# A one-core decoder layer: norm rows of six heads and three groups sent through DRAM, split squares, and four small reorderings

## The chip, the cores and the metric

The kernel runs on one core of a Trainium2 chip. The metric is device time in microseconds from launch to end; three runs of the kernel before gave 1294.66, 1294.87 and 1296.31 us, and the change is compared with their median. The core's engines are TensorE (PE, with its weight loads PEld), VectorE (DVE), ScalarE (ACT), GpSimd (POOL) and SyncE (SP, which here only issues DMAs). ACT and POOL issue DMAs too.

## The reference

One decoder layer on 512 tokens of width 1024, all in float32: a half-weighted SwiGLU FFN, a mixer, cross-attention into 256 memory tokens, a second FFN and a last norm. The change lies in the mixer, whose two halves end in an RMS norm each:

```python
y = y.reshape(bsz, seqlen, SSD_WIDTH) * jax.nn.silu(z.astype(jnp.float32))
yg = y.reshape(bsz, seqlen, SSD_GROUPS, SSD_WIDTH // SSD_GROUPS)
yg = yg * lax.rsqrt(jnp.mean(yg * yg, axis=-1, keepdims=True) + EPS)
y_ssd = yg.reshape(bsz, seqlen, SSD_WIDTH).astype(h.dtype) * ssd_norm_w
...
o = diff_attention(q, k, v, lam, rel_bias)
o = o * lax.rsqrt(jnp.mean(o * o, axis=-1, keepdims=True) + EPS)
y_attn = (o.astype(h.dtype) * subln_w * (1.0 - lambda_init)).reshape(bsz, seqlen, DA_WIDTH)
return jnp.concatenate([y_ssd, y_attn], axis=-1) @ w_out
```

So for each token there is one inverse root per attention head (8 heads, 128 channels each) and one per state-space group (4 groups, 256 channels each). The attention logits also get a bias that depends on the distance of the positions, from a table of 32 buckets for 8 heads.

## The kernel before

Activations lie transposed: a tile is 128 channels (partitions) by 512 tokens in float32. A product in full precision is made of three products in fp32r, a float32 form that TensorE streams one column per step: each operand is split into a high part (a copy rounded to fp32r, on ACT) and a low part (the difference, on DVE), and high x high, high x low and low x high are added up in PSUM. Weights come in by DMA from SP in tiles of 128 x 1024 (`wr`) and are split on the way (`wh`, `wl`, L155 and L156; in the output half of an FFN L1313 and L1315).

A norm needs, for each token, a factor that is the same in all 128 partitions: a row. Tokens are columns, so the kernel makes it in three steps. First a column: the sum of squares over channels for tokens on partitions (128 x 4). Then the inverse root on POOL (a power of -0.5). Then back to a row.

- In a state-space group (`group`, L1020 to L1035) the squares of two tiles are added on DVE. Four plain fp32 products with the 128 x 128 blocks of the squares as stationary operand and one column of ones give `pn` (L1026). `inv_rms_cols` (L363) gives the column. `row_of` (L370) splits the column, multiplies the identity by each half (`ndiag`, two 128 x 512 diagonals, on the engines that are passed in, here POOL for both) and multiplies ones by the diagonals (`nrow`, two products of 512 columns). DVE multiplies the two tiles by the row out of PSUM (L1033).
- In a head (`head`, L843 to L865) the output `of` is transposed in four blocks on TensorE (`ptk`), ACT squares each block and sums it along its free dimension, and since tokens are then on partitions DVE multiplies by the column directly (`on`). Four more transposes (`pot`) bring it back, and the split into `ya` applies the gain of the norm.

The order of the work is planned in the code. `Order` (L57) keeps a clock `t` that counts TensorE's expected time (each `mm`, `transpose` and product adds its share). Dense work, the projections, is a list taken in order; heads, groups, convolutions, the position table and the sums of weights for the second FFN are chains. A chain that does `yield 4.2` is taken up again when the clock has gone 4.2 us further, so that its small products stand between the dense ones; the table `W` holds these delays. Instructions of TensorE, DVE and ACT are placed by the planner of the framework with this order as priority; SP and POOL keep the written order exactly. `behind(list)` holds an instruction behind others in the plan.

Three more places are touched. `prepare` (L630) multiplies the table of biases by a selection matrix (`prel`), copies it (`hot`) and writes it to DRAM from ACT's queue; it runs beside the last third of the first FFN, and ACT's DMA reads it as `bias` for each head. In a group, the products `pf` and `py` of each of two halves wait the delay `gd`. In a head, the products `po` of the weights with the values wait `hs` behind the last transposes. All small tiles share a pool of 55 buffers of 128 x 512. POOL also issues the accumulating DMAs that form sums of weight blocks for the second FFN in DRAM (`block_sums_in_dram`, L1272).

Of the kernel before, what the change touches and what calls it, by code (L numbers as in the profile page):

```python
# [11 lines left out]
F32 = mybir.dt.float32  # L12
R32 = mybir.dt.float32r
AF = mybir.ActivationFunctionType
# [22 lines left out]

W = {"h0": 3.4, "hs": 3.3, "ht": 2.0, "hv": 2.08, "hp": 6.75}
W |= {"g0": 8.28, "gc": 0.75, "gx": 0.92, "gb": 2.59, "gs": 0.51, "gt": 2.0, "gd": 6.9, "gy": 0.38, "gq": 11.8, "gn": 1.5, "gr": 4.4}
W |= {"c0": 4.97, "cs": 3.0, "ct": 4.82}  # L40

SPLIT, AHEAD = 5, 2
# [58 lines left out]
def body(tc, a, dbg=None):  # L101
# [31 lines left out]
    def aux(s, shape=(P, T)):  # L133
        return aux_p.tile(list(shape), F32, tag="aux", name=nm(s))

    def dump(name, t):
        if dbg and name in dbg:
            nc.sync.dma_start(dbg[name], t.bitcast(F32) if t.dtype == R32 else t)
# [24 lines left out]
    def split(s, src, scale=None, half=False, n=T):  # L163
        if half:
            both = s2(s, R32, (P, 2, T // 2))
            hi, lo = both[:, 0], both[:, 1]
        else:
            hi, lo = s2(s + "h", R32, (P, n)), s2(s + "l", R32, (P, n))
        last[:] = [i.ins for i in split_into(hi, lo, src, scale)]
        return hi, lo  # L170
# [192 lines left out]
    def inv_rms_cols(ps, nb, scale, eps):  # L363
# [3 lines left out]
        G.tensor_tensor(col, v, mhalf[:, :nb], ALU.pow)  # L367
        return col

    def row_of(col, nb, first, second, apart):  # L370
        ch = tiny.tile([P, nb], R32, tag="ch", name=nm("ch"))
        first.tensor_copy(ch, col)
        cl = small("cl", nb)
        first.tensor_tensor(cl, col, ch.bitcast(F32), ALU.subtract)
        diags = []
        for eng, c in ((first, ch.bitcast(F32)), (second, cl)):
            diags.append(s2("ndiag", R32, (P, nb, P)))
            eng.tensor_tensor(diags[-1], ident[:, None, :].to_broadcast([P, nb, P]), c[:, :, None].to_broadcast([P, nb, P]), ALU.mult)
        yield apart
        pr = aux("nrow", (P, nb * P))  # L380
        with behind(list(newest_mm)):
            for j in range(2):
                mm(pr, ones_r, diags[j].rearrange("p a b -> p (a b)"), j == 0, j == 1)
        return pr
# [245 lines left out]
    def prepare():  # L630
        rel_far = small("rel_far", 64, bufs=1)[:8]
        V.memset(rel_far, MASKED)
        yield 9.0
        prel = aux("prel", (8, T))
        for i in range(2):
            mm(prel[:, i * H : (i + 1) * H], rel_sb, hot[i], True, True)
        for c in range(T, RW, 64):
            S.dma_start(rel_d[:, c : c + 64], rel_far)
        yield 1.5
        for i in range(2):  # L640
            S.activation(hot[i][:8], prel[:, i * H : (i + 1) * H], AF.Copy, scale=-8.0)
        yield 2.0
        for i in range(2):
            S.dma_start(rel_d[:, i * H : (i + 1) * H], hot[i][:8])
        hot.clear()
# [104 lines left out]
    def backwards(t):  # L750
        n = t.free_size()
        return bass.AP(t.tensor, t.offset + P - 1, [list(t.ap[0]), [P, n // P], [-1, P]])
# [14 lines left out]
    def head(hd, q, kq, bias):  # L767
        es, w0, w1 = {}, {}, {}
        sm = [small("sm", 4) for _ in range(2)]

        def scores(*blocks):
            ps = [aux("ps") for _ in range(2)]
            parts, to = {}, 0
            for i in blocks:
                n = P * (i + 1)
                parts[i] = slice(to, to + n)
                to += n
                for j, (u, w) in enumerate(((0, 0), (0, 1), (1, 0))):
                    for c in range(2):
                        pc = slice(64 * c, 64 * c + 64)  # L780
                        mm(ps[c][:, parts[i]], q[u][pc, i * P : (i + 1) * P], kq[w][pc, :n], j == 0, j == 2)
            for i in blocks:
                n = P * (i + 1)
                es[i] = []
                for c in range(2):
                    ec = s2("ec", shape=(P, n))
                    mn = small("mn", 1, bufs=8)
                    V.tensor_tensor_reduce(out=ec[:, :n], in0=ps[c][:, parts[i]], in1=bias[:, T - n :], scale=0.125, scalar=3e38, op0=ALU.add, op1=ALU.min, accum_out=mn)  # L788
                    S.activation(ec[:, :n], ec[:, :n], AF.Exp, bias=mn, scale=-1.0, accum_out=sm[c][:, i : i + 1])  # L789
                    es[i].append(ec)  # L790

        def combine(i):

            n = P * (i + 1)
            e = es[i]
            rc = small("rc", 1)
            V.reciprocal(rc, sm[1][:, i : i + 1])
            rl = small("rl", 1)
            V.scalar_tensor_tensor(rl, sm[0][:, i : i + 1], nlam, rc, ALU.mult, ALU.mult)
            V.scalar_tensor_tensor(e[0][:, :n], e[1][:, :n], rl, e[0][:, :n], ALU.mult, ALU.add)  # L800
            e.pop()

        def turn(j):
            n = P * (4 - j)
            pt = aux("pt")
            for i in range(j, 4):
                transpose(pt[:, (i - j) * P : (i - j + 1) * P], es[i][0][:, j * P : (j + 1) * P])
            if n <= T // 2:
                both = s2("wt", R32, (P, 2, n))
                w0[j], w1[j] = both[:, 0], both[:, 1]  # L810
            else:
                w0[j], w1[j] = s2("wt", R32, (P, n)), s2("wt", R32, (P, n))
            split_into(w0[j], w1[j], pt[:, :n])

        scores(3)
        yield W["hs"]
        scores(2)
        combine(3)
        yield W["hs"]
        scores(1, 0)  # L820
        combine(2)
        turn(3)
        yield W["hs"]
        combine(1)
        combine(0)
        turn(2)
        yield W["hs"]
        turn(1)
        yield W["ht"]
        turn(0)  # L830
        yield W["hs"]
        es.clear()
        while hd // 4 not in vs:
            yield 1.0
        v = vs[hd // 4]
        hs = slice((hd % 4) * P, (hd % 4 + 1) * P)
        po = aux("po")
        for n, (v_, w_) in enumerate(((0, w0), (1, w0), (0, w1))):
            for j in (0, 1, 2, 3) if n < 2 else (1, 2, 3, 0):
                mm(po[:, j * P :], v[j][v_][:, hs], w_[j], n + j == 0, n == 2 and j == 0)  # L840
        w0.clear()
        w1.clear()
        of = s2("of")  # L843
        S.activation(of, po, AF.Copy)
        yield W["hv"]
        pt = aux("ptk")
        for b in range(4):
            transpose(pt[:, b * P : (b + 1) * P], of[:, b * P : (b + 1) * P])
        ss = small("ss", 4)
        junk = s2("junk", shape=(P, P))  # L850
        for b in range(4):
            S.activation(junk, pt[:, b * P : (b + 1) * P], AF.Square, accum_out=ss[:, b : b + 1])
        ev = small("ev", 4)
        V.scalar_tensor_tensor(ev, sm[0], EPS, sm[0], ALU.mult, ALU.mult)
        V.scalar_tensor_tensor(ev, ss, 1.0 / P, ev, ALU.mult, ALU.add)  # L855
        rr = small("rr", 4)
        G.tensor_tensor(rr, ev, mhalf, ALU.pow)  # L857
        on = s2("on", shape=(P, 4, P))
        V.tensor_tensor(on, pt.rearrange("p (a b) -> p a b", b=P), rr[:, :, None].to_broadcast([P, 4, P]), ALU.mult)
        yield W["hp"]  # L860
        pt = aux("pot")
        for b in range(4):
            transpose(pt[:, b * P : (b + 1) * P], on[:, b])
        ya[hd] = split("ya", backwards(pt), wsub)
        dump(f"ya_{hd}", ya[hd][0])  # L865

    wcv = []
# [61 lines left out]
    def group(g, bt, ct, xs, zs):  # L929
# [52 lines left out]
        for j in range(2):  # L982
# [3 lines left out]
            for hh in range(2):  # L986
# [5 lines left out]
                    S.activation(r[:, c], r[:, c], AF.Relu, bias=cum[:, c, hd : hd + 1], scale=-1.0)  # L992
                S.activation(r, r, AF.Exp, scale=-1.0)
                V.tensor_tensor(r, r, cbm, ALU.mult)
            yield W["gd"] + (W["gt"] if j == 0 else 0.0)
            pf = aux("pf")
            with behind(list(newest_mm)):
                for c in range(1, 4):
# [18 lines left out]
        for j in range(2):  # L1017
# [2 lines left out]
            S.activation(q_, yz[j], AF.Square)  # L1020
            sq.append(q_)
        V.tensor_tensor(sq[0], sq[0], sq[1], ALU.add)
        yield W["gq"] + (1.2 if g == 2 else 0.0)
        pn = aux("pn", (P, 4))
        for b in range(4):
            mm(pn[:, b : b + 1], sq[0][:, b * P : (b + 1) * P], ones[:, 0:1], True, True)  # L1026

        rh = inv_rms_cols(pn, 4, 4.0 / (4 * 256), 4.0 * EPS)
        yield W["gn"]
        pr = yield from row_of(rh, 4, G, G, W["gr"])  # L1030
        for j in range(2):
            n = 2 * g + j
            V.scalar_tensor_tensor(yz[j], yz[j], par[:, C_SSD + n : C_SSD + n + 1], pr, ALU.mult, ALU.mult)  # L1033
            ys[n] = split("ys", yz[j])
            dump(f"ys_{n}", ys[n][0])  # L1035

# [587 lines left out]
```

## Time and profile before

| what | value |
|---|---|
| median of three runs | 1294.87 us |
| profiled execution, its own time | 1296.09 us |
| span of its trace | 1294.1 us |
| TensorE busy | 1281.5 us (99%), 7709 products |
| DVE busy | 971.9 us (75%) |
| ACT busy | 707.6 us (55%) |
| POOL busy | 118.0 us (9%) |
| granted clock of TensorE | 0.997 |
| DMA | 234.75 MB, mean 181 GB/s |

The mixer runs from about 360 to 840 us of the span: heads 0 to 3 at 410 to 494, group 0 at 499 to 551, heads 4 to 7 at 589 to 651, groups 1 to 3 at 655 to 804. A product's width in TensorE's stream is read from the chain of waits in order of time, since the ends of products in the trace are modelled and overlap. "Idle before" in brackets names what an engine waited for.

### The profile page before, as it was taken

What the parts mean: (1) busy time and instruction counts of PE and PEld (TensorE: products, weight loads), DVE (VectorE), ACT (ScalarE), POOL (GpSimd) and SP (SyncE); (2) the same over time, 40 slices, a digit from 0 to 9 for tenths busy, and PEclk for the clock granted to TensorE, in tenths of its full rate; (3) what the DMA queues carried; (4) which work ended last, traced back from release to release, by engine and by line L of the source; (5) the groups of instructions that cost most, each with busy time, mean ns of one, the idle gap of its engine ahead of it and who ended that gap; (6) DMA issues with size and microseconds to landing.
All of it is one profiled execution on the core that took longest, in us unless ns stands there. A gap on an engine that the chain in (4) does not pass through costs nothing.

```text
span 1294.1 us, 20089 instructions
## 1 busy us (share of the span) xinstructions
PE 1281.5 (99%) x7709; PEld 1123.7 (87%) x7709; DVE 971.9 (75%) x1549; ACT 707.6 (55%) x1203; POOL 118.0 (9%) x149
## 2 busy tenths in 40 slices
PE   9999999999999999999999999999999999999997
PEld 7889998998988778877888888889899999989995
DVE  6988898797876686567868696645678868877886
ACT  7545564565654564447644574435466646555554
POOL 1001010001101011101102011020001000000000
PEclk9999999999999999999999999999999999999998
DMA  9368677788875436653476567593249876666662
GB/s 331 101 170 209 187 199 199 226 208 227 272 232 155 131 66 169 224 163 96 107 211 187 151 163 227 193 234 107 66 132 255 210 221 184 191 189 190 180 201 92
DMA packets 69551, 234.75 MB, mean 181 GB/s; under 512 B 8192, under 2 KB 9696, under 8 KB 69104
## 3 DMA queue, kind: packets, MB, share of 16 engines
q1 hardware_dynamic: 53488, 180.91, 42.2%
q0 software_dynamic: 13168, 45.67, 19.9%
q10 hardware_dynamic: 2800, 6.91, 1.7%
q8 instruction: 60, 0.98, 0.3%
q14 instruction: 35, 0.29, 0.1%
HBM read 231.30 MB, written 48.29 MB: 216 GB/s over the span
## 4 chain that ended last, share of the span: by engine, by line
PE 82%; issue 12%; DMA 2%; ACT 1%; DVE 1%; POOL 1%; POOLq 0%; SPq 0%; ACTq 0%
PE qb L243 12%; PE pm L146 10%; PE qe L243 8%; PE qa L243 8%; PE pxbc L146 5%; PE ob L1327 5%; PE oa L1327 4%; PE oe L1327 4%; PE pcq L146 3%; PE pz L146 3%; PE pa L146 2%; PE pk L146 2%; PE pq L146 2%; PE pcv L146 2%; PE pv L146 2%
## 5 line engine op out<-in xcount | busy, mean ns | idle before, releaser
L155 ACT ACTIVATE wh<-wr 128x1024 fp32r<-128x1024 f32 (+1 forms) x245 | 251.2, 1028 | 235.2 <-PE qe L243 27.9
L156 DVE TENSOR_TENSOR wl<-wr,wh 128x1024 fp32r<-128x1024 f32 (+1 forms) x245 | 290.8, 1188 | 83.5 <-ACT wh L155 61.3
L1313 ACT ACTIVATE wh<-wr 128x1024 fp32r<-128x1024 f32 (+1 forms) x78 | 76.9, 987 | 68.4 <-PE ob L1327 19.5
L1315 DVE TENSOR_TENSOR wl<-wr,wh 128x1024 fp32r<-128x1024 f32 (+1 forms) x78 | 87.5, 1131 | 15.0 <-ACT wh L1313 13.1
L789 ACT ACTIVATE ec<-ec,mn 128x512 f32<-128x512 f32 (+3 forms) x64 | 35.4, 554 | 21.9 <-DVE mn L788 21.9
L788 DVE CUSTOM_DVE_ANT_0 ec<-ps,bias 128x512 f32<-128x512 f32 (+3 forms) x64 | 28.1, 486 | 14.8 <-PE ps L146 14.7
L252 POOL DMA_DIRECT2D wr<-in_f2q x11 | 9.7, 881 | 309.8 <-DMA wr<-in_f2q 156.2
L902 DVE SCALAR_TENSOR_TENSOR conv<-pxbc,par,conv 128x511 f32<-128x511 f32 (+2 forms) x48 | 35.7, 745 | 2.3 <-ACT conv L898 1.5
L367 POOL TENSOR_TENSOR ncol<-nv,mhalf 128x4 f32<-128x4 f32 (+1 forms) x9 | 9.7, 1077 | 294.1 <-DVE nv L365 266.5
L146 PE MATMUL pxbc<-hnl,wh 128*128 128x512 f32 x128 | 35.4, 403 | 0.0
L146 PE MATMUL pxbc<-hnh,wh 128*128 128x512 f32 x128 | 35.3, 400 | 0.0
L146 PE MATMUL pxbc<-hnh,wl 128*128 128x512 f32 x128 | 32.3, 393 | 0.0
L454 DVE TENSOR_TENSOR gate<-qb,row 128x512 f32<-128x512 f32 x19 | 13.2, 692 | 22.1 <-PE qb L243 22.1
L146 PEld LDWEIGHTS pxbc<-hnh,wl 128*128 128x128 f32 x128 | 23.8, 188 | 5.3 <-issue 0.3
L252 POOL DMA_DIRECT2D wr<-in_f1q x16 | 14.0, 875 | 152.8 <-DMA wr<-in_f1q 49.8
L146 PEld LDWEIGHTS pxbc<-hnl,wh 128*128 128x128 f32 x128 | 23.3, 188 | 4.8 <-issue 0.4
L146 PEld LDWEIGHTS pxbc<-hnh,wh 128*128 128x128 f32 x128 | 23.2, 189 | 4.5 <-issue 0.3
L455 ACT ACTIVATE gate<-gate 128x1024 f32<-128x1024 f32 x19 | 20.1, 1056 | 10.9 <-DVE gate L454 10.9
L146 PE MATMUL pv<-wh,hnh 128*128 128x512 f32 x64 | 25.3, 395 | 0.0
L146 PE MATMUL pv<-wh,hnl 128*128 128x512 f32 x64 | 25.2, 393 | 0.0
L155 ACT ACTIVATE s24h<-s 128x512 fp32r<-128x512 f32 x30 | 18.8, 627 | 9.0 <-DVE s L214 8.9
L857 POOL TENSOR_TENSOR rr<-ev,mhalf 128x4 f32<-128x4 f32 x8 | 8.3, 1035 | 161.3 <-DVE ev L855 161.3
(465 smaller groups left out, 3546.9 us busy)
## 6 DMA issues: line engine op xcount, KB each, us to landing
wr<-in_f2q SPq DMA_DIRECT2D x44, 512.0 KB, 4.8
wr<-in_f1q SPq DMA_DIRECT2D x40, 512.0 KB, 4.5
wr<-in_f1b SPq DMA_DIRECT2D x23, 512.0 KB, 5.7
isum<-in_f2q SPq DMA_DIRECT2D x22, 512.0 KB, 5.8
wr<-isum SPq DMA_DIRECT2D x22, 512.0 KB, 4.0
wsum<-in_f2b SPq DMA_DIRECT2D x20, 512.0 KB, 6.3
wr<-wsum SPq DMA_DIRECT2D x20, 512.0 KB, 4.7
wr<-in_f1q POOLq DMA_DIRECT2D x16, 512.0 KB, 7.2
```

The costliest lines, as they stand in the source:

```text
L146: newest_mm[:] = [nc.tensor.matmul(out, w, x, start=start, stop=stop).ins]
L155: S.activation(hi, src, AF.Copy),
L156: V.tensor_tensor(lo, src, hi.bitcast(F32), ALU.subtract),
L243: newest_mm[:] = [nc.tensor.matmul(out, w_[:, wc], xs[kp][which][x_], start=first and j == 0 and f == 0 and kp == 0, stop=j == 2 and kp == ...
L252: last_sum[:] = [G.dma_start(raw, m, accum_op=ALU.add).ins]
L455: S.activation(gate, gate, AF.Silu)
L788: V.tensor_tensor_reduce(out=ec[:, :n], in0=ps[c][:, parts[i]], in1=bias[:, T - n :], scale=0.125, scalar=3e38, op0=ALU.add, op1=ALU.min, ...
L789: S.activation(ec[:, :n], ec[:, :n], AF.Exp, bias=mn, scale=-1.0, accum_out=sm[c][:, i : i + 1])
L902: V.scalar_tensor_tensor(y[:, d:], ps[:, : T - d], par[:, cw + j : cw + j + 1], y[:, d:], ALU.mult, ALU.add)
L1313: high = S.activation(hi, raw, AF.Copy)
L1315: low = V.tensor_tensor(lo, raw, hi.bitcast(F32), ALU.subtract)
L1327: newest_mm[:] = [nc.tensor.matmul(ps, a_[:, ts], b_[:, ws], start=first and k == 0 and j == 0, stop=k == n - 1 and j == 2, skip_group_che ...
```

## The change

- Heads 0 to 2 and 4 to 6 (`hd % 4 < 3`) go to a new function `normed_far`: ACT squares the untransposed output, the square is split in fp32r, and eight products of two columns of ones with its blocks give the column of sums (`pon`). The power on POOL follows; then the column (128 x 4) is written to DRAM by a DMA from POOL, read back 8 us later by a second one that gives all 512 values to each partition (`row_by_dram`), and 12 us after that DVE multiplies `of` by gain and row. The eight transposes go. Heads 3 and 7 stay as they were, with their `po` 0.8 us later.
- All groups split the added squares and use eight such products in place of four in plain fp32. Groups 0 to 2 take the row through DRAM in place of diagonals and `nrow`. Group 3 keeps the diagonals, on DVE in place of POOL, and its `nrow` stands 0.8 us earlier.
- Group 2's second `pf`/`py` stand 0.5 us later.
- The position table's products stand 4 us later, and the copies of them are held behind the last split of weights.

```diff
+W |= {"hn": 4.2, "rw": 8.0, "rr": 12.0}
...
+    def row_by_dram(col, landed, read):
+        there = dram.tile([P, 4], F32, name=nm("there"))
+        G.dma_start(there, col)
+        yield landed
+        row = s2("far")
+        G.dma_start(row, bass.AP(there.tensor, there.offset, [[0, P], [1, 4 * P]]))
+        yield read
+        return row.rearrange("p (t b) -> p b t", b=4)
+
+    def blocks(t):
+        return t.rearrange("p (b t) -> p b t", b=4)
...
-        yield 9.0
+        yield 13.0
         prel = aux("prel", (8, T))
...
-        for i in range(2):
-            S.activation(hot[i][:8], prel[:, i * H : (i + 1) * H], AF.Copy, scale=-8.0)
+        with behind(list(recent)):
+            for i in range(2):
+                S.activation(hot[i][:8], prel[:, i * H : (i + 1) * H], AF.Copy, scale=-8.0)
...
-        yield W["hs"]
+        yield W["hs"] + (0.8 if hd % 4 == 3 else 0.0)
...
         S.activation(of, po, AF.Copy)
+        if hd % 4 < 3:
+            yield from normed_far(hd, of, sm[0])
+            return
...
+    def normed_far(hd, of, sums):
+        sq = s2("osq")
+        S.activation(sq, of, AF.Square)
+        sq = split("osq", sq)
+        yield W["hn"]
+        pon = aux("pon", (P, 4, 2))
+        for b in range(4):
+            for j in range(2):
+                mm(pon[:, b], sq[j][:, b * P : (b + 1) * P], ones_r[:, 0:2], j == 0, j == 1)
+        ev = small("ev", 4)
+        V.scalar_tensor_tensor(ev, sums, EPS, sums, ALU.mult, ALU.mult)
+        V.scalar_tensor_tensor(ev, pon[:, :, 0], 1.0 / P, ev, ALU.mult, ALU.add)
+        rr = small("rr", 4)
+        G.tensor_tensor(rr, ev, mhalf, ALU.pow)
+        row = yield from row_by_dram(rr, W["rw"], W["rr"])
+        on = s2("on")
+        V.scalar_tensor_tensor(blocks(on), blocks(of), wsub, row, ALU.mult, ALU.mult)
+        ya[hd] = split("ya", backwards(on))
...
-            yield W["gd"] + (W["gt"] if j == 0 else 0.0)
+            yield W["gd"] + (W["gt"] if j == 0 else 0.5 if g == 2 else 0.0)
...
+        sq = split("ysq", sq[0])
         yield W["gq"] + (1.2 if g == 2 else 0.0)
-        pn = aux("pn", (P, 4))
+        pn = aux("pn", (P, 4, 2))
         for b in range(4):
-            mm(pn[:, b : b + 1], sq[0][:, b * P : (b + 1) * P], ones[:, 0:1], True, True)
-
-        rh = inv_rms_cols(pn, 4, 4.0 / (4 * 256), 4.0 * EPS)
-        yield W["gn"]
-        pr = yield from row_of(rh, 4, G, G, W["gr"])
+            for j in range(2):
+                mm(pn[:, b], sq[j][:, b * P : (b + 1) * P], ones_r[:, 0:2], j == 0, j == 1)
+
+        rh = inv_rms_cols(pn[:, :, 0], 4, 4.0 / (4 * 256), 4.0 * EPS)
+        if g < 3:
+            pr = yield from row_by_dram(rh, W["rw"], W["rr"])
+        else:
+            yield W["gn"]
+            pr = blocks((yield from row_of(rh, 4, V, V, W["gr"] - 0.8)))
```

More of the change, by code (lines that the diff above doesn't have):

```diff
@@ L1022, in group @@
         V.tensor_tensor(sq[0], sq[0], sq[1], ALU.add)
+        sq = split("ysq", sq[0])
         yield W["gq"] + (1.2 if g == 2 else 0.0)
[L1024 removed]
+        pn = aux("pn", (P, 4, 2))
         for b in range(4):
[L1026 to L1030 removed]
+            for j in range(2):
[6 more added lines that the diff above has]
+            pr = blocks((yield from row_of(rh, 4, V, V, W["gr"] - 0.8)))
         for j in range(2):
             n = 2 * g + j
[L1033 removed]
+            V.scalar_tensor_tensor(blocks(yz[j]), blocks(yz[j]), par[:, C_SSD + n : C_SSD + n + 1], pr, ALU.mult, ALU.mult)
             ys[n] = split("ys", yz[j])
```

1 line of the change is left out of this document (added).

## The prediction, made before the change was run

> **What bounds the kernel now.** I read the page's busy table first, then the table of stretches, then the chain in order of time through the heads and the groups, and last the timeline around the few places where TensorE stands.
>
> ```profile
> span 1294.1 us, 20089 instructions
> PE 1281.5 (99%) x7709; PEld 1123.7 (87%) x7709; DVE 971.9 (75%) x1549; ACT 707.6 (55%) x1203; POOL 118.0 (9%) x149
> ```
>
> ```profile
> 560.00:650.00 90.00, 90.00 (x490) 71.31 (x490) 67.09 (x178) 53.14 (x145) 9.99 (x11) 1.00 0.42 110
> ```
>
> The second fence is the stretch with heads 4 to 7 (columns: PE, PEld, DVE, ACT, POOL busy with counts, granted clock, DMA share, GB/s). TensorE is busy in all of its 90 us at granted clock 1.00, while DVE works 67.09/90 = 75%, ACT 59% and POOL 11%. So an instruction taken off TensorE shortens the kernel by its place in TensorE's stream, an instruction taken off the others only by what TensorE now waits for them, and the price of everything the change adds to DVE, ACT, POOL and DMA is nothing until it makes TensorE late.
>
> **What TensorE pays for the parts that are exchanged.** The chain in order of time gives each part's width in TensorE's stream (start, width, what):
>
> ```profile
> 517.70 1.02 PE py L146 x16
> ...
> 592.34 0.44 PE ptk L150 x4
> ...
> 599.75 0.44 PE pot L150 x4
> ...
> 689.99 7.71 PE pxbc L146 x34
> 697.70 0.79 PE pn L146 x8
> 698.49 3.34 PE pxbc L146 x14
> ...
> 705.46 0.46 PE nrow L146 x2
> ```
>
> A 512-column product in the stream is 7.71/34 = 0.227 us. One head pays ptk and pot, 2 x 0.44 = 0.88 us. A group's pn is 0.79 us, and the 14 products behind it take 3.34 where 14 x 0.227 = 3.18 were due, so 0.79 + 0.16 = 0.95 us in all. Its nrow is 0.46 us.
>
> The new sums are eight products of two columns against 128x128 pieces of a square split in two fp32r tiles, for six heads and four groups alike. No product of that form is in the trace. What bounds it is the load of its stationary tile:
>
> ```profile
> L146 PEld LDWEIGHTS pn<-ones,ysq x32: 187/192/193, 540.2 to 795.2; 128*128 128x128 f32 x32
> L146 PEld LDWEIGHTS pm<-ysh,wh x64: 186/188/189, 792.0 to 833.5; 128*128 128x128 f32 x64
> L146 PEld LDWEIGHTS prel<-hot,rel_sb x4: 80/84/85, 310.5 to 310.9; 32*8 32x8 f32 x4
> ```
>
> An eight-column load takes 84 ns, a 128-column load 188 to 192, whether the tile is plain fp32 (ysq) or fp32r (wh): (188 - 84)/120 = 0.87 ns a column, 0.11 us for 128. The old pn is 32 records for 16 products, two loads each, and its eight records in 0.79 us stand 0.10 us apart, near that load and not near the one column that they stream. The new form has eight loads too. So I price the new sums at eight loads, 8 x 0.11 = 0.88 us. Bounds: above, the old pn's 0.95; below, py, whose sixteen products stand 1.02/16 = 0.064 us apart, so 8 x 0.064 = 0.51 us.
>
> The Trainium skill's page "TensorE: Matmul & The Clock Gate", section "Back-to-back issue gap", gives products of 1 to 64 columns about 60 cycles, 25 ns. By that alone the ten sums would cost an estimated 80 x 0.025 = 2.0 us; the pn row's 0.10 us contradicts it, and the same page's section "LDWEIGHTS (loading the stationary operand)" makes 128/1.2 = 107 ns of the load, with which the rows agree.
>
> Terms on TensorE, then:
> - Heads 0 to 2 and 4 to 6: minus 0.88, plus 0.88, six times: 0 (+0.4 at worst, -2.2 at best). Eight loads go for eight loads.
> - Groups 0 to 3: the fp32 pn goes, the split one with as many loads comes: 0 (4 x (0.51 - 0.95) = -1.8 at best).
> - Groups 0 to 2: nrow goes: 3 x -0.46 = -1.4 us. This is the only part of the exchange that surely shortens the stream: TensorE's instructions should go from 7709 to 7709 - 6 = 7703.
>
> **The four reorderings.** The timeline shows four places where TensorE really stands; each is what one small edit touches.
>
> ```profile
> 311.79 1.09 PE L1327 MATMUL oe<-wl,s31h 128*128 128x512 f32 x4
> 313.74 1.20 PE L1327 MATMUL ob<-wh,s24h 128*128 128x512 f32 x4 [0.86 <-ACT wh L1313]
> ```
>
> ```profile
> 311.56 0.64 ACT L641 ACTIVATE hot<-prel 8x256 f32<-8x256 f32 x2 [1.55 <-PE prel L146]
> 311.97 0.62 ACTq L644 DMA_DIRECT2D rel_d<-hot  x2
> 312.63 2.01 ACT L1313 ACTIVATE wh<-wr 128x1024 fp32r<-128x1024 f32 x2 [0.43 <-DVE wr L1365]
> ```
>
> ```profile
> 481.26 0.39 PE L146 MATMUL pxbc<-hnh,wh 128*128 128x512 f32 x1
> 482.04 0.86 PE L146 MATMUL po<-wt,vh 128*128 128x512 f32 x4 [0.39 <-ACT wt L155]
> ```
>
> ```profile
> 744.61 1.07 PE L146 MATMUL pz<-hnh,wl 128*128 128x512 f32 x4
> 745.84 0.88 PE L146 MATMUL py<-th,xdt 128*64 128x128 f32 x12 [0.16 <-DVE th L994]
> ```
>
> ```profile
> 801.83 2.41 PE L146 MATMUL pm<-ysh,wh 128*128 128x512 f32 x8
> ```
>
> The lost time is the next start less the last start and its due products. ob: 313.74 - (311.79 + 4 x 0.227) = 1.04 us. po of head 3: 482.04 - (481.26 + 0.23) = 0.55 us. py of group 2: 745.84 - (744.61 + 0.91) = 0.32 us. pm behind group 3's row: eight products, due in about 1.07 + 4 x 0.227 = 1.98, take 2.41: 0.43 us. Sum 2.3 us.
> - Position table: ACT waits 1.55 us for prel, copies it, issues two DMAs for 0.62 us, and only then splits the weights for ob. With prel 4 us later and the copies held behind that split, the 1.04 us goes; should the 0.43 us in that row be a true wait for DVE, 0.6 at least. The copies and the 0.62 us of issues come later on ACT, where they stand before other splits: 0 to 0.62 us comes back, I take 0.2. The table's first reader is the first head, well behind the first FFN, so lateness there costs nothing.
> - Head 3's products 0.8 us later, group 2's second product 0.5 us later: other products stand in front, 0.55 and 0.32 us are filled.
> - Group 3's diagonals go from POOL to DVE, 0.8 us earlier: -0.43 us.
>
> I credit all four, less 0.2: -2.1 us.
>
> **What lies beside TensorE.**
>
> ```profile
> L155 ACT ACTIVATE ysh<-y x8: 619/632/636, 549.7 to 803.5; 128x512 fp32r<-128x512 f32 x8
> L156 DVE TENSOR_TENSOR ysl<-y,ysh x8: 682/693/693, 550.4 to 804.1; 128x512 fp32r<-128x512 f32 x8
> ```
>
> Per head ACT drops four squares with their sums and gains one square and one copy; even without the four, 2 x 0.63 = 1.3 us a head lie in its idle 41%. DVE gains one subtraction, 0.69 us: 6 x 0.69 over the heads' stretches, covered by its idle quarter. From po to the sum the chain is now copy, square, split high, split low: 3 x 0.63 + 0.69 = 2.6 us, against a delay of 4.2: it fits unless the queues add 1.6 us. In a group 0.63 + 0.69 = 1.3 us come between the added squares and pn. In group 2 that is tight:
>
> ```profile
> 751.69 0.68 DVE L1022 TENSOR_TENSOR ysq<-ysq,ysq 128x512 f32<-128x512 f32 x1
> ...
> 754.18 0.95 PE L146 MATMUL pn<-ones,ysq 128*128 128x1 f32 x8
> ```
>
> The sum is ready at 752.37 and used at 754.18, 1.8 us, less 1.3 leaves 0.5, less than one more DVE instruction ahead in the queue. I put +0.3 us there (0 to 1.3).
>
> The row's way through DRAM is a pow, a write, a wait on POOL, a read and one DVE product:
>
> ```profile
> L857 POOL TENSOR_TENSOR rr<-ev,mhalf 128x4 f32<-128x4 f32 x8 | 8.3, 1035 | 161.3 <-DVE ev L855 161.3
> ```
>
> ```profile
> isum<-isum POOLq DMA_DIRECT2D x11, 512.0 KB, 9.4
> ...
> bias<-rel_d ACTq DMA_DIRECT2D x8, 256.0 KB, 3.9
> ```
>
> ```profile
> hb<-in_hb POOLq DMA_DIRECT2D x1, 16.0 KB, 7.2
> ```
>
> (Last column: us from issue to landing.) POOL does the pow in 1.04; the small write lands within 7.2, as hb does; the read of 256 KB in 3.9 to 9.4, as the bias rows or as a slow POOL transfer: at most 17.6 us and two issues, against 8 + 12 = 20 of allowance. The read waits on POOL for the write; behind it stand the accumulating DMAs, due only in the second FFN, and the next head's pow, which comes a head later. The result is needed late:
>
> ```profile
> 620.16 1.91 PE po L146 x12
> ...
> 660.23 2.29 PE pm L146 x10
> ```
>
> Head 6's po ends at 622.07; 4.2 + 20 later is 646.3, and its first reader, pm, starts at 660.23: 14 us of cover. Without that cover each row would cost what it is late. POOL loses the diagonals and gains two DMA issues a row; it is busy 11% of the stretch, so either is covered.
>
> **Sum.** 0 + 0 - 1.4 - 2.1 + 0.3 = -3.2 us; at the lower bounds of the sums it is -3.2 - 2.2 - 1.8 = -7.2, with the upper bounds of the heads, the table's wait and issues, and group 2 it is -3.2 + 0.4 + 0.4 + 0.4 + 1.0 = -1.0. The profiled execution took 1296.09 us, 2.0 above its span and 1.2 above the median of the three runs (1294.87). Against its own time: 1292.9; carried to the median: 1291.7.
>
> **Rivals.**
> - *Cheap small products.* If loads of fp32r tiles with little to stream run at py's pace or better, the time is 1294.87 - 7.2 = 1287.7. For it: py's row. Against: equal loads for wh and ysq. One in ten. The Trainium skill's issue gap, cited above, is this rival's rule.
> - *The waits come back elsewhere.* All delays are counted on the planner's own clock and ten blocks change their cost in it, so the order of all three queues shifts from 310 to 800 us. The four stalls found sum to 2.3 us; as many new ones leave the nrow term alone, 1293.5. For it: group 2's 0.5 us, the issues on ACT. Against: only four such stalls in the whole middle now. Three in ten.
> - *Late rows.* Landings at the upper ends, 7.2 + 9.4, with the pow and about 1 us of issue for each are 19.6 us; behind a POOL held by an accumulating DMA they pass 20. Then the row's product stands at the head of DVE's in-order queue with the weight splits behind it, and ACT's and DVE's splits come late. Nine rows, each 1 us late on TensorE, are +9 - 3.2 = +5.8: 1300.7; it decides from 3.2/9 = 0.36 us a row. The longer life of the held head output, split square and row in the pool of 55 buffers works the same way (a DMA waits for a buffer); no row shows its price. For it: 9.4. Against: 14 us of cover, DMA share 0.42. One in ten. The Trainium skill's page "DMA: Bandwidth & Descriptors", section "Specifications", says that pieces under 512 bytes are read, modified and written; the column is written in 16-byte pieces, and no DMA of before has them.
>
> **Chances and range.** Forecast, half: 1291.7, own range 1289.5 to 1293.9 (the bound of -1.0 above, half of the way to the cheap products below). The other halves: 0.1, 0.3, 0.1. Faster by over 0.2% (2.6 us, about what a measurement of this kernel can tell from no change) holds for most of the forecast (0.38), all of the cheap products (0.1) and a little of the returning waits (0.05): 0.53. Slower: late rows and the worst of the waits, 0.11. The same: 0.36. The range runs from the cheap products' 1287.7, rounded to 1287.5, to 1295.5, 2 us above the returning waits' 1293.5, since as many waits again may come.
>
> **What would show it.** TensorE with 7703 instructions; pon's eight products 0.8 to 1.0 us wide, as pn's; ob, po, py and pm without a gap at the four places; DVE waiting on no DMA for the row; pm after heads and groups starting no later than other work allows. The prediction is wrong if pon is under 0.6 us wide, if new gaps of over 0.3 us stand on TensorE between 310 and 800 us, or if DVE idles on a row's landing.

## The result, and the profile after

The changed kernel takes 1300.78 us (median of six runs, 1299.48 to 1303.38) against 1294.82 us for the kernel before (six runs, 1294.65 to 1296.31). The ratio is 1.0045, with a 95% interval of 1.0035 to 1.0056: slower by 6 us, where 3 us less were forecast. The profiled execution took 1300.17 us by its own time, 4.1 more than that of before. Three runs of the experiments below (one each of the reorderings alone, the heads alone and the mixture) took 4492, 1801 and 2114 us; they count in the medians given there, but not in the ratios.

The page of the kernel after, its span and busy times:

```profile
span 1298.4 us, 20080 instructions
PE 1282.8 (99%) x7703; PEld 1124.4 (87%) x7703; DVE 980.4 (76%) x1563; ACT 707.7 (55%) x1171; POOL 118.9 (9%) x151
```

TensorE has the 7703 instructions that were forecast. Its waits say where it stood (kernel after; columns: who, for whom, us in total, times, longest):

```profile
PE pq L147 <- DVE vl L157: 2.7, 1, 2.7
...
PE qb L244 <- DVE c L311: 1.2, 1, 1.2
PE ob L1369 <- ACT wh L1355: 1.1, 1, 1.1
PE pm L147 <- DVE x L913: 0.7, 1, 0.7
PE pbt L151 <- DVE nv L366: 0.3, 1, 0.3
```

The longest is new, and it is at the row of group 0. The timeline there, all engines (start, width, what, and in brackets the idle time before it and its releaser):

```profile
541.95 0.16 DVE L366 TENSOR_SCALAR nv<-pn 128x4 f32<-128x4 f32 x1 [3.87 <-PE pn L147]
542.19 1.03 POOL L368 TENSOR_TENSOR ncol<-nv,mhalf 128x4 f32<-128x4 f32 x1 [47.84 <-DVE nv L366]
542.82 1.23 DVE L157 TENSOR_TENSOR wl<-wr,wh 128x1024 fp32r<-128x1024 f32 x1 [0.71 <-PE pv L147]
543.53 0.64 POOL L373 DMA_DIRECT2D there<-ncol  x1 [0.30 <-POOL ncol L368]
547.88 0.57 POOL L376 DMA_DIRECT2D far<-there  x1 [3.71 <-ACT wh L156]
552.38 2.20 DVE L1075 SCALAR_TENSOR_TENSOR y<-y,par,far 128x512 f32<-128x512 f32 x2 [8.33 <-DMA far<-there]
554.48 1.23 DVE L157 TENSOR_TENSOR wl<-wr,wh 128x1024 fp32r<-128x1024 f32 x1
555.61 1.89 DVE L157 TENSOR_TENSOR vl<-pv,vh 128x512 fp32r<-128x512 f32 x3
```

DVE finishes one weight split at 544.05 and then stands 8.33 us: next in its queue are the products by the row (`y`), and the row has not landed. The power was done at 543.22, the write was issued at 543.53, the read at 547.88, and the row is there at 552.38: 10.3 us from the end of `nv` at 542.11 to the product. Behind `y` in the queue stand the next weight split and the low halves of the values (`vl`), and TensorE needs those next (`pq` does not read `vl`: the kernel has four accumulators in PSUM for such products, and `vl` must first have read `pv` out of the one that `pq` takes). The kernel before, DVE in the same stretch:

```profile
547.79 1.23 DVE L156 TENSOR_TENSOR wl<-wr,wh 128x1024 fp32r<-128x1024 f32 x1 [4.24 <-DMA wr<-in_wq]
548.93 1.40 DVE L1033 SCALAR_TENSOR_TENSOR y<-y,par,nrow 128x512 f32<-128x512 f32 x2
...
551.64 2.00 DVE L156 TENSOR_TENSOR vl<-pv,vh 128x512 fp32r<-128x512 f32 x3
```

There `y` runs at 548.93, behind the weight split that it now stands ahead of, and `vl` at 551.64; after, `vl` starts 4.0 us later. What it costs TensorE is in its own rows of the kernel after, same stretch:

```profile
553.02 0.61 PE L147 MATMUL pv<-wl,hnh 128*128 128x512 f32 x2
556.36 3.36 PE L147 MATMUL pq<-hnh,wh 128*128 128x512 f32 x8 [2.73 <-DVE vl L157]
559.53 2.38 PE L147 MATMUL pq<-hnl,wh 128*128 128x512 f32 x8
561.74 1.53 PE L147 MATMUL pq<-hnh,wl 128*128 128x512 f32 x6
```

Two products from 553.02 were due to end at 553.02 + 2 x 0.227 = 553.47; the next starts at 556.36, 2.9 us late. The following sixteen take 561.74 - 556.36 = 5.38 us where 16 x 0.227 = 3.63 were due: another 1.75 us, without any wait. The table of stretches of the kernel after says why (columns as in the prediction; the granted clock is the third number from the end):

```profile
553.00:556.00 3.00, 0.64 (x3) 0.19 (x1) 3.00 (x4) 1.54 (x2) 0.81 (x1) 1.00 0.96 202
556.00:558.00 2.00, 1.64 (x5) 1.32 (x6) 2.00 (x4) 0.00 (x0) 0.00 (x0) 0.72 0.89 137
558.00:560.00 2.00, 2.00 (x7) 1.52 (x6) 1.24 (x2) 0.00 (x0) 0.00 (x0) 0.50 1.21 373
560.00:562.00 2.00, 2.00 (x10) 1.62 (x9) 0.00 (x0) 0.06 (x1) 0.00 (x0) 0.93 0.84 340
```

Read as half speed for a part of each stretch, the clock is at 0.50 for (1 - 0.72) x 2/0.5 = 1.1 us of the second, all of the third and 0.3 us of the fourth, 3.4 us from soon after TensorE takes up work again. So one late row costs 2.9 + 1.75 = 4.65 us, more than the whole difference of the two spans, 1298.4 - 1294.1 = 4.3.

The other places, kernel after. Group 2's sums and what follows them on TensorE:

```profile
761.10 0.25 PE L147 MATMUL pn<-ones_r,ysqh 128*128 128x2 f32 x1
...
761.88 0.25 PE L147 MATMUL pn<-ones_r,ysql 128*128 128x2 f32 x1
762.39 0.55 PE L151 MATMUL pbt<-ident,th 128*128 128x128 f32 x3 [0.26 <-DVE nv L366]
763.64 0.72 PE L147 MATMUL pm<-yah,wh 128*128 128x512 f32 x2 [0.70 <-DVE x L913]
```

The sums stand (761.88 - 761.10)/7 = 0.11 us apart, as priced. Behind them TensorE loses 762.39 - 761.88 - 0.11 = 0.40 us, and behind the three transposes 763.64 - 762.39 - 3 x 0.11 = 0.9, so 1.3 us in all. The place after the position table, on TensorE and on ACT:

```profile
312.45 1.02 PE L147 MATMUL prel<-hot,rel_sb 32*8 32x256 f32 x4
314.61 0.73 PE L1369 MATMUL ob<-wh,s24h 128*128 128x512 f32 x2 [1.13 <-ACT wh L1355]
```

```profile
313.50 2.27 ACT L1355 ACTIVATE wh<-wr 128x1024 fp32r<-128x1024 f32 x2 [1.14 <-DVE wr L1407]
```

The wait ahead of `ob`, 0.86 us before, is 1.13 now; ACT no longer waits for `prel`, it waits for DVE. Of the other three gaps of before, those at head 3's `po` (0.39) and group 2's `py` (0.16) are gone from the list of waits.

### The profile page after: what moved, and what is told of

It reads as the page before. It is cut to its first block, busy times and chain, and to the rows that moved or that the text cites. A ratio compares the mean times of both kernels' runs of the same rounds, so it can differ in the third digit from the quotient of the medians.

```text
span 1298.4 us, 20080 instructions
## 1 busy us (share of the span) xinstructions
PE 1282.8 (99%) x7703; PEld 1124.4 (87%) x7703; DVE 980.4 (76%) x1563; ACT 707.7 (55%) x1171; POOL 118.9 (9%) x151
## 4 chain that ended last, share of the span: by engine, by line
PE 56%; DVE 1%; ACT 0%; issue 0%; POOLq 0%; POOL 0%; DVEq 0%; ACTq 0%
PE pm L147 8%; PE qb L244 7%; PE pxbc L147 5%; PE qe L244 5%; PE qa L244 5%; PE pcq L147 3%; PE ob L1369 3%; PE pz L147 3%; PE oa L1369 2%; PE oe L1369 2%; PE pq L147 2%; PE pk L147 2%; PE pcv L147 2%; PE pcs L147 1%; PE pco L147 1%; PE ps L147 1%
## 5 line engine op out<-in xcount | busy, mean ns | idle before, releaser
L156 ACT ACTIVATE s24h<-s 128x512 fp32r<-128x512 f32 x30 | 18.8, 626 | 10.2 <-DVE s L215 10.2
L156 ACT ACTIVATE s31h<-s 128x512 fp32r<-128x512 f32 x30 | 18.7, 625 | 7.2 <-DVE s L213 4.2
```

The source lines that it names most:

```text
L156: S.activation(hi, src, AF.Copy),
```

## The experiments

The kernels of one batch ran on one chip beside the kernel before, whose medians there were 1295.25, 1295.24 and 1295.35 us (31, 27 and 23 runs). Ratios are to it, with a 95% interval.

**The product by the row held behind the splits** (kernel after, groups 0 to 2). `recent` and `last` are the last splits that the plan holds at that point.

```diff
+            with behind(recent + last if g < 3 else []):
                 V.scalar_tensor_tensor(blocks(yz[j]), blocks(yz[j]), ...)
```

> The changed kernel with one edit: in groups 0 to 2 the DVE products that read the row from DRAM are held, in the plan, behind the latest weight split and the latest split of a projection. DVE's queue then has them behind the splits of the values in group 0 instead of ahead of them. Theory (place in DVE's queue): the product of group 0 stood at the head of DVE's queue for 8.3 us until the row landed, the splits behind it came late, TensorE stood 2.9 us at 553 us and then ran nine products at half clock for another 1.8; all of that goes: about 1300.8 - 4.7 = 1296.1 us, no gap near 553, granted clock 1.00 there. Rival (the DMAs or the strided rows themselves slow the kernel, wherever the product stands): time stays within 1 us of 1300.8, the gap only moves.

Measured: 1294.22 us, ratio 0.9991 [0.9981, 1.0000]. DVE's timeline of this kernel:

```profile
552.72 0.69 DVE L157 TENSOR_TENSOR vl<-pv,vh 128x512 fp32r<-128x512 f32 x1 [0.67 <-ACT vh L156]
554.14 1.23 DVE L157 TENSOR_TENSOR wl<-wr,wh 128x1024 fp32r<-128x1024 f32 x1 [0.73 <-ACT wh L156]
...
560.69 1.12 DVE L1076 SCALAR_TENSOR_TENSOR y<-y,par,far 128x512 f32<-128x512 f32 x1
```

The splits now pass, `y` finds its row there at 560.69, and TensorE does not stand. Row, DMAs and split squares are all still in place; only the place of the products in DVE's queue differs, and 6.6 us come back by the medians (0.9991 against 1.0045 by the ratios, each to the kernel before beside it). That names the cause. The waits at group 2 and at `qb` stay.

**Group 0's row back on diagonals** (kernel after, on POOL as before the change).

```diff
-        if g < 3:
+        if g in (1, 2):
             pr = yield from row_by_dram(rh, W["rw"], W["rr"])
         else:
             yield W["gn"]
-            pr = blocks((yield from row_of(rh, 4, V, V, W["gr"] - 0.8)))
+            e, d = (V, 0.8) if g == 3 else (G, 0.0)
+            pr = blocks((yield from row_of(rh, 4, e, e, W["gr"] - d)))
```

> The changed kernel with group 0 alone taken back to diagonals on POOL and two products of 512 columns. Theory: the same gap goes, 0.46 us of products come back: about 1300.8 - 4.7 + 0.5 = 1296.6 us. Rival (nine rows each cost something): only a ninth of the loss goes, about 1300 us.

Measured: 1292.88 us, 0.9984 [0.9975, 0.9994]: a gain over both kernels, and 3.7 us more than expected. Besides the stand at 553 us, the wait at `qb` near 1000 us is gone too, and that ahead of `ob` is 0.2; why these two went is not shown.

**The four reorderings alone** (kernel before).

```diff
-        yield 9.0
+        yield 13.0
...
-        for i in range(2):
-            S.activation(hot[i][:8], ...)
+        with behind(list(recent)):
+            for i in range(2):
+                S.activation(hot[i][:8], ...)
...
-        yield W["hs"]
+        yield W["hs"] + (0.8 if hd % 4 == 3 else 0.0)
...
-            yield W["gd"] + (W["gt"] if j == 0 else 0.0)
+            yield W["gd"] + (W["gt"] if j == 0 else 0.5 if g == 2 else 0.0)
...
-        pr = yield from row_of(rh, 4, G, G, W["gr"])
+        pr = yield from (row_of(rh, 4, V, V, W["gr"] - 0.8) if g == 3 else row_of(rh, 4, G, G, W["gr"]))
```

> The kernel before with only the four reorderings (position table, head 3, group 2's second product, group 3's diagonals on DVE and 0.8 us earlier). The prediction's terms: -2.1 us, 1292.7. By the changed kernel's trace, where the gaps at po and py are gone but those at ob and at pm are not: -0.55 - 0.32, 1293.9. Rival (the planner puts other waits in their place): 1294.8 or above.

Measured: 1294.49 us, 0.9992 [0.9982, 1.0002]. The gaps at `po` and `py` are filled, the one ahead of `ob` is not. Of `pm`'s 0.43 us 0.25 are left: ten products from 801.54 to 804.06 us, 2.52 where 10 x 0.227 = 2.27 were due. ACT's row there:

```profile
312.75 2.26 ACT L1314 ACTIVATE wh<-wr 128x1024 fp32r<-128x1024 f32 x2 [1.14 <-DVE wr L1366]
```

The split that `ob` needs starts at 312.75 with the copies out of its way, and started at 312.63 with the copies in front of it: DVE's sum of weights `wr` released it in both. The 1.55 us that ACT waited for `prel` in the kernel before was time in which it would have waited for DVE anyway.

**The six heads' new norm alone** (kernel before).

```diff
+        if hd % 4 < 3:
+            yield from normed_far(hd, of, sm[0])
+            return
```

> The kernel before with only the six heads' norms taken through split squares and DRAM. The prediction's term: eight loads for eight loads, 0 us, 1294.8 within 1 us. Rival (the strided rows, 1.12 us on DVE, and the late landings make DVE late in the heads): 1296.5 or more, with gaps on TensorE between 415 and 655 us.

Measured: 1296.12 us, 1.0005 [0.9995, 1.0014], no new gap over 0.3 us on TensorE. Eight loads for eight loads, and six rows through DRAM that nobody waits for, come out at nothing that can be measured.

**Group 2's sums still later** (the first experiment with one more delay).

```diff
-        yield W["gq"] + (1.2 if g == 2 else 0.0)
+        yield W["gq"] + (2.7 if g == 2 else 0.0)
```

> The kernel with the held rows (e1_hold_y) and group 2's sums 1.5 us later on the planner's clock. In its trace TensorE stands 0.39 us behind pn of group 2 (a transpose waits for pn's bank) and 0.86 us behind that (products wait for a DVE addition). Theory (the split of the squares makes pn late in group 2 and pulls DVE's work with it): both gaps go, 1294.2 - 1.25 = 1293.0 us. Rival (DVE is full there whatever the place of pn): the gaps only move, 1294.2.

Measured: 1294.45 us, 0.9994 [0.9985, 1.0003], as without it. The loss at the sums shrinks, but another place pays (TensorE of this kernel; the profiled execution, 1297.84 us, was the longest of the eleven):

```profile
783.23 0.98 PE L147 MATMUL py<-th,xdt 128*64 128x128 f32 x14 [1.53 <-DVE th L1031]
```

Group 3's first `py` now waits 1.53 us for DVE. In this trace the loss moved with the order; by the time nothing was gained.

**Without the edit of the position table** (the second experiment less that edit: `yield 9.0`, and no hold).

> The kernel with group 0 on diagonals (e2_g0_diag) less the edit of the position table. By the prediction's term the edit is worth 0.8 us: 1292.9 + 0.8 = 1293.7. By the traces the gap ahead of ob stays with the edit, since ACT's split there waits for DVE's sums and these for weights that land late: 1292.9 within 0.4.

Measured: 1293.45 us, 0.9984 [0.9976, 0.9993], the same ratio as with it (1292.88 us). Whatever the edit is worth is below what can be told here; in the profiles of the kernels that have it, TensorE's wait ahead of `ob` is 1.0 to 1.1 us in five, 0.2 in one and none in one (the column in order), without it 0.9 in all.

**The split squares alone** (kernel before, all groups, rows by diagonals as before).

```diff
+        sq = split("ysq", sq[0])
...
-        pn = aux("pn", (P, 4))
+        pn = aux("pn", (P, 4, 2))
         for b in range(4):
-            mm(pn[:, b : b + 1], sq[0][:, b * P : (b + 1) * P], ones[:, 0:1], True, True)
+            for j in range(2):
+                mm(pn[:, b], sq[j][:, b * P : (b + 1) * P], ones_r[:, 0:2], j == 0, j == 1)
```

> The kernel before with only the squares of the four groups split and the sums made by eight fp32r products; rows by diagonals as before. The prediction's terms: 0 for the products, +0.3 for group 2, 1295.5. By the changed kernel's trace group 2 costs 1.25 us: 1296.5. Cheap small products would give 1293.5.

Measured: 1296.04 us, 1.0005 [0.9996, 1.0014]: 0.8 us more by the medians, between the 0.3 of the prediction and the 1.3 that the trace of the kernel after shows at group 2. The interval holds both, and nothing too. The trace tells more. Behind group 2's sums TensorE goes on at once:

```profile
755.86 0.25 PE L146 MATMUL pn<-ones_r,ysql 128*128 128x2 f32 x1
755.97 0.33 PE L150 MATMUL pxt<-ident,th 128*128 128x128 f32 x1
```

Neither wait of the kernel after (`pbt` for `nv`, `pm` for `x`) is among this kernel's waits. So the split by itself does not make the 1.3 us. Other work stands between the sums and `pbt` here; in the kernel after `pbt` follows the sums directly. Which of the other edits brings that about is not shown.

**Group 0's row alone through DRAM** (the kernel before, its sums in plain fp32 as they were, with that one row, not held).

```diff
-        pr = yield from row_of(rh, 4, G, G, W["gr"])
+        if g == 0:
+            pr = yield from row_by_dram(rh, W["rw"], W["rr"])
+        else:
+            yield W["gn"]
+            pr = blocks((yield from row_of(rh, 4, G, G, W["gr"])))
```

> The kernel before with one edit: group 0's row alone goes through DRAM, not held. Theory (place in DVE's queue): this one row loses what the changed kernel lost near 553 us, 2.9 us of standing and 1.8 us at half clock, less its two products of 512 columns: 1295.2 + 4.7 - 0.5 = 1299.4. Rival (the loss needs the heads' rows and their DMAs beside it): 1295 to 1296.

Measured: 1302.41 us (1302.09 to 1302.78), 1.0052 [1.0038, 1.0065]. One row of nine is 7.2 us by itself. DVE's row of this kernel, and its stretches:

```profile
554.44 2.16 DVE L1049 SCALAR_TENSOR_TENSOR y<-y,par,far 128x512 f32<-128x512 f32 x2 [9.99 <-DMA far<-there]
```

```profile
553.00:556.00 3.00, 1.04 (x5) 0.54 (x3) 1.56 (x2) 1.86 (x3) 0.00 (x0) 1.00 0.96 160
556.00:558.00 2.00, 0.00 (x0) 0.00 (x0) 2.00 (x3) 0.00 (x0) 0.00 (x0) 0.56 0.86 196
558.00:560.00 2.00, 1.60 (x4) 1.32 (x5) 2.00 (x4) 0.00 (x0) 0.00 (x0) 0.50 0.60 202
560.00:562.00 2.00, 2.00 (x7) 1.52 (x6) 1.27 (x2) 0.00 (x0) 0.00 (x0) 0.50 0.48 141
```

The row lands later than in the kernel after (6.4 us from the read's issue, there 4.5), TensorE stands longer (4.5 us, from 553.88 to 558.40), and the half clock lasts until 563.1 us: the next sixteen products take 2.3 us more than their due.

**The planner told to read the row 8 us later** (kernel after).

```diff
-W |= {"hn": 4.2, "rw": 8.0, "rr": 12.0}
+W |= {"hn": 4.2, "rw": 8.0, "rr": 20.0}
```

> The changed kernel with the planner's delay behind the row's read raised from 12 to 20 us for all nine rows. Theory (this delay does not set where DVE takes the product: the planner puts it into DVE's queue where it takes the row as landed, still ahead of the splits of the values): no help, the product of group 0 waits some 8 to 10 us again, 1300 to 1302 us. Rival (the allowance of 20 us from sum to row was only too short): the gap goes as with the held rows, about 1294 to 1295.

Measured: 1303.91 us, 1.0064 [1.0051, 1.0077]. DVE's timeline:

```profile
542.61 1.23 DVE L157 TENSOR_TENSOR wl<-wr,wh 128x1024 fp32r<-128x1024 f32 x1 [0.71 <-PE pv L147]
551.51 2.18 DVE L1075 SCALAR_TENSOR_TENSOR y<-y,par,far 128x512 f32<-128x512 f32 x2 [7.68 <-DMA far<-there]
```

`y` still follows the same weight split and still waits 7.68 us. So for this row the delay in the chain is no allowance: it does not set the instruction's place in DVE's queue. In the heads it does: the first head's product starts 12.1 us behind the issue of the row's read in the kernel after (423.38, 435.47) and 25.6 us behind it here (422.08, 447.71). Why the two differ is not settled.

TensorE now stands 2.2 us ahead of `pq`, at full clock afterwards (first row of the second fence), and anew 2.2 us near 798 for `cvl`, with the half clock afterwards (second row):

```profile
799.91 2.90 PE L147 MATMUL pm<-ysh,wh 128*128 128x512 f32 x6 [2.06 <-DVE cvl L161]
```

```profile
556.00:558.00 2.00, 2.00 (x10) 1.63 (x10) 2.00 (x4) 0.00 (x0) 0.00 (x0) 1.00 0.69 140
800.00:802.00 2.00, 2.00 (x5) 1.63 (x6) 1.88 (x3) 0.55 (x1) 1.77 (x3) 0.50 0.84 260
```

This and smaller new waits (1.4 us in two for `x`, 0.7 for `st`, 0.5 for `osql`) cost more than the shorter stand at `pq` saves.

**A mixture of the parts that paid** (rows of groups 0 and 1 through DRAM and held, groups 2 and 3 with plain sums and diagonals, the heads' new norm, the small reorderings without the table's).

```diff
-        if g < 3:
+        if g < 2:
             pr = yield from row_by_dram(rh, W["rw"], W["rr"])
...
+            with behind(recent + last if g < 2 else []):
```

> What the runs leave standing, in one kernel: the changed kernel with the rows of groups 0 and 1 held, groups 2 and 3 on plain fp32 sums and diagonals (group 2's on POOL, group 3's on DVE 0.8 us earlier), and the position table as before. Against e2_g0_diag (1292.9): group 2's gaps of 1.25 us and the 0.28 behind group 3's row go; a row of group 0 goes (-0.46) and one of group 2 comes (+0.46): about 1291.5. If group 2's gaps were not the split's: 1292.5 to 1293.

Measured: 1293.21 us, 0.9981 [0.9973, 0.9990]. It beats both kernels; the experiment with group 0 on diagonals does as well within the intervals. The time is nearer to the 1292.5 to 1293 of the second case than to 1291.5: the waits behind group 2's sums are gone from the trace, but a new one of 0.36 us (`pxt` for DVE's `th`) stands 4.6 us further on.

**The column written so that the row lies in order** (the first experiment; the write goes in pieces of 4 bytes, and DVE reads the row with step one).

```diff
-        G.dma_start(there, col)
+        G.dma_start(bass.AP(there.tensor, there.offset, [[1, P], [P, 4]]), col)
...
-        return row.rearrange("p (t b) -> p b t", b=4)
+        return row.rearrange("p (b t) -> p b t", b=4)
```

> The kernel with the held rows (e1_hold_y), but the column is written to DRAM block by block, in pieces of 4 bytes, so that DVE reads the row contiguously and no longer in steps of four elements. DVE's product by the row should fall from 1.12 to about 0.74 us, as by the row in PSUM before; if the step is not the cause it stays at 1.12. The write should take longer to land than 1.8 us. Time as e1_hold_y, 1294.2 within 1 us, since DVE's work is covered.

Measured: 1300.9 us, 1.0043 [1.0030, 1.0056], a miss. The products did become shorter (first fence, by the tile of the row; min, median, max in ns), but the write became slow (second fence, DMAs with the median us from issue to landing in the last column), and the longest wait on TensorE follows from it (third):

```profile
L900 DVE SCALAR_TENSOR_TENSOR on<-of,wsub,far x6: 744/752/753, 438.0 to 654.5; 128x512 f32<-128x512 f32 x6
```

```profile
there<-rr POOLq DMA_DIRECT2D x6, 2.0 KB, 10.2
there<-ncol POOLq DMA_DIRECT2D x3, 2.0 KB, 10.3
```

```profile
PE pt L151 <- DVE ec L814: 4.0, 1, 4.0
```

It is the same loss at another place, now in a head: ahead of `ec` in DVE's queue the product of an earlier head waits 4.30 us for its row, and the half clock follows (437.5 to 444.3 us).

```profile
437.96 0.75 DVE L900 SCALAR_TENSOR_TENSOR on<-of,wsub,far 128x512 f32<-128x512 f32 x1 [4.30 <-DMA far<-there]
```

**The mixture with all heads on transposes.**

```diff
-        if hd % 4 < 3:
-            yield from normed_far(hd, of, sm[0])
-            return
```

> e10_mixed with all eight heads on transposes as in the kernel before (head 3 and 7 still 0.8 us later). By the prediction's term (eight loads for eight loads) and e4_heads_only (+0.6 us at most): the same as e10_mixed within 0.8 us. If the heads' new way is worth something with the other parts in place: 1 to 2 us slower than e10_mixed.

Measured: 1294.88 us, 0.9994 [0.9985, 1.0002], 1.7 us above the mixture by the medians. The two ran beside each other, and the runs of the mixture that its ratio rests on end at 1293.84 us where those of this kernel begin at 1293.97, so the difference is clear. But the traces do not put it into the heads: `prel`, ahead of all heads, starts 1.4 us later than in the mixture (311.6 against 310.2), 0.5 of it from a second wait at an `ob` in the first FFN, and the last `pn`, behind all heads, 1.1 us later (795.3 against 794.2). So what makes the difference stays open; alone the heads' new norm was worth nothing.

## Why the prediction was wrong, point by point

- **Row through DRAM, costed at nothing: wrong, and this is the step that failed.** It read "at most 17.6 us and two issues, against 8 + 12 = 20 of allowance". The size held: 10.3 us from sum to product, of it 3.8 for the write to land and 4.5 for the read. The allowance was none for this row. The two delays rank the chain in the plan; the kernel with 12 made 20 shows the same place in DVE's queue for `y`, while the heads' products moved on. That the planner puts the product wherever its own model has DVE idle and takes the row as landed is argued from this, not shown. The cover was wrong too: the 14 us ahead of `pm` is the distance to the row's last reader in TensorE's order, while what mattered was the instruction behind `y` in DVE's queue. The trace of before held the answer: `y` ran at 548.93 and `vl`, needed at once, at 551.64, while the loads of `pn` began at 540.2 (its row stands in the prediction). With the sum at about 542, a way of more than 7 us makes DVE stand, and the prediction itself allowed for 17.6.
- **"Late rows" was the rival that happened, mis-sized.** Its sentence on the head of DVE's queue describes the trace. It was priced as nine rows at 1 us each, and that its 1300.7 us lie so near the measured 1300.78 is luck. In fact eight rows came in time (in the heads the products stand 12 to 18 us behind the read's issue), and one cost 4.65 us in the trace and 7.2 by itself. It also left out that a stand of TensorE can be paid again by the clock, 1.75 us here. One chance in ten was too little for a queue whose contents had not been looked at.
- **Heads, 0: right for the part alone.** The kernel with it is at 1.0005 [0.9995, 1.0014]. The 1.7 us by which the mixture without it is slower are not traced to the heads.
- **Sums, 0, and "cheap small products": the first right, the rival wrong.** All loads of the new sums (kernel after) are as long as the old ones:

```profile
L147 PEld LDWEIGHTS pon<-ones_r,osqh x24: 186/192/192, 417.6 to 632.0; 128*128 128x128 f32 x24
```

  They stand 0.11 us apart, as the prediction made of a load of 128 columns, so the load is taken to set the pace. The Trainium skill, "TensorE: Matmul & The Clock Gate", section "LDWEIGHTS (loading the stationary operand)", has a load take its columns over 1.2, 107 ns for 128, with which this agrees. The 25 ns for so few columns in its section "Back-to-back issue gap" are the gap of single products; the same section says that in a stream of loads and products both set the spacing, so the rival read it too far.
- **`nrow`, -1.4: the six instructions are gone**, 7709 to 7703. Its time was not measured by itself.
- **The four reorderings, -2.1: `po` and `py` right, `ob` and `pm` wrong.** With them alone the ratio is 0.9992, about 1 us, which its interval does not tell from nothing. The 1.04 us ahead of `ob` hung on DVE's `wr`, as the prediction allowed for ("should the 0.43 us in that row be a true wait for DVE, 0.6 at least") and then did not take. `pm` keeps 0.25 of its 0.43 us with the reorderings alone and all of it in the kernel after (ten products from 806.70 to 809.40 us, 2.70 where 2.27 were due); why is not settled.
- **Group 2, +0.3 (0 to 1.3): mis-sized, and its reason is not borne out.** The kernel after loses 1.3 us there, the upper bound, with TensorE waiting for `nv` and for `x`, both on DVE. But with the split squares alone neither wait appears, so the split's 1.3 us of work on ACT and DVE do not cause them by themselves.
- **"Waits come back elsewhere": right as a kind.** The wait at `qb`, 1.0 to 1.2 us near 1000 us, is in the five kernels in which the rows of all three groups go through DRAM (the kernel after, the held one, that with later sums, the later read, the column in order) and in none of the others. What links the two is not settled.

Without the late row (first experiment) the kernel came to 1 us under the one before, against 3.2 forecast: group 2 costs 1.0 more than its term, the table gives 0.8 less, `pm` 0.4 less, and `qb` takes 1.2. These four make 3.4 us where 2.2 are missing; the interval of that kernel's ratio is about 1.2 us to either side.

## What to carry to other kernels

When a value is moved to a slower way, look up in the trace what stands behind its first reader in that reader's own in-order queue, and when that is needed; the slack of the value's last use says nothing about it. A delay in a plan that ranks instructions is no guarantee that a transfer has landed: where it must not block, the reader itself has to be held behind the work that may not wait. And where a gap has a releaser, ask for the one next in line before the gap is credited: the split ahead of `ob` started within 0.12 us of the same time with its named cause gone.

## What the runs showed of the hardware

- A stand of TensorE can cost more than its length. After 2.9 us without a product the granted clock is 0.50 for 3.4 us (stretches of the kernel after); with group 0's row alone TensorE stands 4.5 us and the clock is 0.50 for 6.8 us, 556.2 to 563.1, of which the last 4.7 have products. The length of the stand does not settle it: of two stands of 2.2 us in the kernel with the later read, one is followed by full clock and one by 3.4 us at 0.50. The Trainium skill, "TensorE: Matmul & The Clock Gate", section "What's actually happening", has the same half rate after an idle window of about 3.4 us; the stands of 2.2 and 2.9 us were shorter than that.
- DVE pays for the stride of this row. In the kernel after it reads the row in steps of four elements (tile of the row; min, median, max in ns; the groups' products take 1.14 us), first fence; in the kernel before it read a row in order out of PSUM, second fence:

```profile
L900 DVE SCALAR_TENSOR_TENSOR on<-of,wsub,far x6: 1117/1123/1135, 435.5 to 654.0; 128x512 f32<-128x512 f32 x6
```

```profile
L1033 DVE SCALAR_TENSOR_TENSOR y<-y,par,nrow x8: 736/740/747, 548.9 to 802.7; 128x512 f32<-128x512 f32 x8
```

  1.12 us against 0.74, and 0.75 with the row in order in SBUF (the experiment with the column in order): the step makes the difference, not the memory.
- 2 KB written in 512 pieces of 4 bytes land 10.2 us after their issue; in 128 pieces of 16 bytes, in the kernel after, 1.8 us after it (median of nine; group 0's 3.8). The Trainium skill, "DMA: Bandwidth & Descriptors", section "Specifications", says that pieces under 512 bytes are read, modified and written, and gives no price there; no run here shows that mechanism, only that four times as many pieces, each a quarter as long, took over five times as long.
